# Ten adaLN rows of a two-layer trunk: sum over the partitions by accumulating transfers instead of matmuls with ones

## The chip, the cores and the metric

The kernel runs on one core of a Trainium2 chip. The metric is device time in microseconds (us), the median of the runs. Engines are written PE (TensorE), DVE (VectorE), ACT (ScalarE), POOL (GpSimd) and SP (SyncE). A DMA is issued by an engine, in the order of that engine's program; here SP and POOL issue them.

## The reference

512 tokens of 1024 values pass through two layers; layer 0 mixes tokens by stick-breaking attention, layer 1 by a gMLP, and each is followed by a SwiGLU FFN of width 2816. Around each of these four sub-layers stand two RMS norms, scaled and shifted by rows that are computed from one conditioning vector c:

```python
def ada_modulation(c, w, b):
    m = jax.nn.silu(c) @ w + b
    shift, scale, gate = jnp.split(m, 3, axis=-1)
    ...
for i in range(DEPTH):
    shift, scale, gate = ada_modulation(c, mix_ada_w[i], mix_ada_b[i])
    h = rms_norm(x, mix_pre_g[i]) * (1.0 + scale) + shift
    ...
    x = x + gate * rms_norm(y, mix_post_g[i])
    shift, scale, gate = ada_modulation(c, ffn_ada_w[i], ffn_ada_b[i])
    h = rms_norm(x, ffn_pre_g[i]) * (1.0 + scale) + shift
    y = swiglu(h, ffn_w_gate[i], ffn_w_up[i], ffn_w_down[i])
    x = x + gate * rms_norm(y, ffn_post_g[i])
```

The change concerns the product silu(c) @ w + b: rows of 1024 values (shift, scale, gate), each a sum over 1024 rows of w.

## The kernel before

**Layout of the work.** Everything in fp32 goes through PE as three matmuls of rounded halves (high by high, high by low, low by high; `mm3`). Weights are loaded by SP, their high half wh is rounded by ACT, the low half wl is the difference, by DVE. The split pairs lie in a pool of five (`wpool`), so they are made ahead of their use. There are stages: the v, k and q products with attention in between (to about 205 us), the output projection of attention (to 265), the first FFN's gate and up products (`Ffn.seven`, a seven-product scheme per block), its down projection (`out_proj` with steps = 2; about 490 to 605), the gMLP (`gmlp`, to about 760), and the second FFN (`seven`, then `last`). Between the sub-layers stands `boundary(s, tt, ...)`: for each 128 tokens it multiplies by the row G (gate times post gain), adds to x, multiplies by A ((1 + scale) times pre gain) and adds B (shift), then transposes on PE for the next sub-layer.

**The rows.** Ten rows G, A, B for the boundaries are made while other work runs, by the class `Bg` (L313). For boundary 0 they are G0, A0, B0, made during attention, with their loads issued by POOL; G1 is made in the first FFN's `seven` loop, A1, B1 and G2 in its down projection, A2 there and in the gMLP, B2 in the gMLP, and G3 in the second FFN's `seven` loop; these loads are issued by SP. (The first sub-layer's shift and scale are made at the start in another way.) For one row, `Bg.run` does this: POOL clears a tile acc of 128 x 1024 and the bias row is loaded into its partition 0. Then eight times: 128 rows of w are loaded (rawada, 512 KB) and DVE adds them, each scaled by its silu(c) value, to acc (`ada_stt`, L306, a SCALAR_TENSOR_TENSOR). What is left is the sum of acc over its 128 partitions, wanted on every partition.

**The sum over partitions, before.** In halves of 512 columns, acc is split (acch on ACT, accl on DVE) and two matmuls with a matrix of ones, `ones_r`, add up the partitions and put the sum on all of them at once (L369, L370). For 10 rows that is 10 x 2 x 2 = 40 matmuls. Their results stand in PSUM under the names spare (during attention) and adaps. From there G is multiplied by g, and A becomes (1 + sum) times g, both on DVE, g being a gain row that SP loads broadcast to 128 partitions; B is copied by ACT.

**The order of work.** `Bg.run` is a generator. The host stages call `bg.step()` at fixed places, and each step issues the next piece, so the place in each engine's order is set by hand. During attention PE, DVE and ACT run strictly in written order (`chain`); elsewhere the framework's scheduler places instructions by their dependences, and each engine then issues in order. In `out_proj` with steps the bank of y[0] is needed for adaps: the accumulation of y[0] is broken at k = `mid` = 13, ACT copies its first part to yp, the matmuls with ones of A1, B1, G2 all stand after that place, and DVE adds yp back at the end. From k = 13 a second object, bg2, makes A2. `slot` (L47) gives tiles of 4 KB a partition from a pool of 28.

Of the kernel before, what the change touches and what calls it, by code (L numbers as in the profile page):

```python
# [8 lines left out]
F32 = mybir.dt.float32  # L9
# [16 lines left out]
def trunk(ctx: ExitStack, tc: tile.TileContext, A: dict, out: bass.AP):  # L26
# [2 lines left out]
    consts = ctx.enter_context(tc.tile_pool(name="consts", bufs=1))  # L29
    wraw = ctx.enter_context(tc.tile_pool(name="wraw", bufs=2))  # L30
    wpool = ctx.enter_context(tc.tile_pool(name="wpool", bufs=5))
    adas = ctx.enter_context(tc.tile_pool(name="adas", bufs=1))
    npool = ctx.enter_context(tc.tile_pool(name="npool", bufs=2))
    small = ctx.enter_context(tc.tile_pool(name="small", bufs=4))
    s4 = ctx.enter_context(tc.tile_pool(name="s4", bufs=28))
# [277 lines left out]
    class Bg:  # L313
# [5 lines left out]
        def __init__(self, *parts, slots=False, queue=nc.sync):  # L319
            self.slots = slots  # L320
            self.queue = queue
            self.bank = lambda: bank("adaps", "p")

            self.parts = [
                (n, int(s), int(s) + (n != "G"), {"G": 2, "A": 1, "B": 0}[n]) for n, s in parts
            ]
            self.gen = self.run()
            self.todo = [(s, part, k) for _, _, s, part in self.parts for k in range(KD)]
            self.raws = []
# [8 lines left out]
        def run(self):  # L338
            for name, at, s, part in self.parts:
                acc = slot(F32, name, 1, D)[:, 0, :]  # L340
                ada[name, at] = acc
                nc.gpsimd.memset(acc, 0.0)
                load(acc[0:1, :], A["adab"][s, part], self.queue)
                for k in range(KD):
                    if self.slots:
                        raw = slot(F32, "rawada", 1, D)[:, 0, :]
                        load(raw, A["ada"][s, part, k])
                        yield
                    else:
                        self.ahead(1 + (k + 1 < KD or name != self.parts[-1][0]))  # L350
                        raw = self.raws.pop(0)
                    ada_stt(acc, raw, k)
                    if not self.slots:
                        yield
            for name, at, s, part in self.parts:
                acc = ada[name, at]
                if part:
                    row = A["pre_g"] if part == 1 else A["post_g"]
                    g = slot(F32, "g", 1, D)[:, 0, :]
                    load(g, row[s : s + 1, :].to_broadcast([P, D]))  # L360
                for b in range(2):
                    c = slice(b * 512, (b + 1) * 512)
                    h = adas.tile([P, 512], F32R, tag="acch", name=nm("acch"))
                    l = adas.tile([P, 512], F32R, tag="accl", name=nm("accl"))
                    split(h[:], l[:], acc[:, c])
                    yield
                    yield
                    ps = self.bank()
                    mm(ps[:], ones_r, h[:], True, False, last_tp[0])  # L369
                    mm(ps[:], ones_r, l[:], False, True)  # L370
                    if part == 0:
                        act.activation(acc[:, c], ps[:], AF.Copy)
                    elif part == 1:
                        dve.scalar_tensor_tensor(acc[:, c], ps[:], 1.0, g[:, c], ALU.add, ALU.mult)
                    else:
                        dve.tensor_tensor(acc[:, c], ps[:], g[:, c], ALU.mult)

        def step(self, n=1):

            while n and next(self.gen, self) is not self:  # L380
                n -= 1
            return n

    def rms(part, first=None):

# [107 lines left out]
    def out_proj(s, nk, get_act, wkey, J, bg, hT, nxt=(), pre=None, S=None, steps=0, bg2=None):  # L493

        last = 0 if steps else 3
        mid = min(nk - J, -(-8 * len(bg.parts) // steps) + 1) if steps else None  # L500
        yp = None
        y = [[None, None] for _ in range(NT)]

        def step(k, tt, a, w, halves=(0, 1)):
            for hf in halves:
                if k == 0 or k == mid and tt == last:
                    y[tt][hf] = bank("y", "p" if tt == last else "b")
                mm3(
                    y[tt][hf][:],
                    a[0][:, tt * P : (tt + 1) * P], a[1][:, tt * P : (tt + 1) * P],  # L510
                    w[0][:, 0, hf * 512 : (hf + 1) * 512],
                    w[1][:, 0, hf * 512 : (hf + 1) * 512],
                    k == 0 or k == mid and tt == last, k == nk - 1 or k + 1 == mid and tt == last,
                )

        npre = 0
        if pre is not None:
            npre = len(pre["w"])
            for tt in pre["y"]:
                y[tt] = pre["y"][tt]  # L520
        for k in range(nk - J):
            a = get_act(k)
            w = pre["w"][k] if k < npre else wget(wkey(k))
            for tt in range(NT):
                if k >= npre or tt not in pre["y"]:
                    step(k, tt, a, w)
            bg.step(steps)
            if bg2 is not None and mid is not None and k >= mid:
                bg2.step(1)
            if k + 1 == mid:  # L530
                yp = slot(F32, "yp")
                for hf in range(2):
                    act.activation(yp[:, hf, :], y[last][hf][:], AF.Copy)
                bg.step(99)
        bg.step(99)
        tail = [
            (k, get_act(k), wget(wkey(k), J + 1 if k == nk - J else 0))
            for k in range(nk - J, nk)
        ]
        sqrt_table()  # L540
        xs = {tt: x_load(tt) for tt in range(2)}
        xin = xs.get
        for tt in range(NT):
            for hf in range(2):
                for k, a, w in tail:
                    step(k, tt, a, w, (hf,))
            if tt == last and yp is not None:
                for hf in range(2):
                    dve.tensor_tensor(yp[:, hf, :], y[tt][hf][:], yp[:, hf, :], ALU.add)
                y[tt] = [yp[:, hf, :] for hf in range(2)]  # L550
            if tt < 2:
                boundary(s, tt, y[tt], xin, hT, S, "p" if last == 0 else "b")
                xs[tt + 2] = x_load(tt + 2)
        evacs, late = [], []
        for n, tt in enumerate((2, 3)):
            if nxt:
                evacs.append(nxt[n]())
            late.append(boundary(s, tt, y[tt], xin, hT, S, "p" if tt == 3 else "b"))
        if nxt:
            dve.gate, act.gate = ready[0], last_sqrt[0]  # L560
            late[0][1]()
            evacs.append(nxt[2]())
# [195 lines left out]
    with tc.tile_pool(name="att", bufs=1) as att, tc.tile_pool(name="att2", bufs=6) as att2:  # L758
# [192 lines left out]
        bg.bank = None  # L951
        cur = attend(0)
        for k in range(KD):
            if k % 2 == 0:
# [8 lines left out]
        v_evac(vb, 1)  # L963
        tw = [bank("tw") for _ in range(2)]
        av = bank("av")
        spare = bank("spare")
        bg.bank = lambda: spare
        dve.chain = act.chain = True
        fill(6)
        cur[0](B0)  # L970
# [2 lines left out]
        for i in range(NPAIR):  # L973
# [6 lines left out]
            def rest():  # L980
                n, sums = next(F)
                fill(n)
                bg.step(sums)

            for group, js in zip((LATE, *EARLY), (B31, B2, B0)):
                flip(group, 0)
# [11 lines left out]
                step_v(i - 2)  # L998
        for _ in fgen:
            bg.step(1)  # L1000
        bg.step(99)
        pe["chain"] = dve.chain = act.chain = False

# [14 lines left out]
    class Ffn:  # L1018
# [81 lines left out]
        def run(self, bg0, bg, bg2, steps, nhT, nxt, nS=None):  # L1100
            for f in range(NH):
                self.unit(f, 256, 256)()
            for f in range(NH, KF):
                self.seven(f)()
                if f % 3:
                    bg0.step(1)
            bg0.step(99)
            if self.li == 1:
                return self.last()
            out_proj(  # L1110
                self.s, KF, lambda k: act_split(self.act[k // 2][:, k % 2, :]),
                lambda k: ("wdown", self.li, k), 4, bg, nhT, nxt, None, nS, steps, bg2,
            )


        def last(self):
# [113 lines left out]
            for half in range(2):  # L1230
# [3 lines left out]
                tail = items[-NLAST:] if half else []  # L1234
                while n < len(items) and items[n][0] == half and items[n] not in tail:
                    ahead(n)
                    _, kind, j = items[n]
                    n += 1
                    if kind == "o":
# [77 lines left out]
    def gmlp(bg, hT, nhT, nS, nxt):  # L1317
# [96 lines left out]
                    )  # L1414

        for m in range(KD):
            mix(m)
            sp.append(act_split(u4[m // 2][:, m % 2, :]))
            if m >= 4:
                part(m - 4)  # L1420
# [104 lines left out]
```

## Time and profile before

| what | value |
| --- | --- |
| median of three runs | 1125.85 us (1125.52 to 1125.99) |
| the profiled execution, its own time | 1127.71 us |
| its span in the profile | 1125.9 us |
| mean granted clock of PE | 0.998 |
| PE, DVE, ACT, POOL busy | 98%, 80%, 54%, 4% |
| HBM read, written | 164.43 MB, 8.39 MB |

The span runs from the first to the last instruction; the 1.8 us between it and the execution's time lie around it. The busy shares are means over stages with different limits. A row of the timeline gives start, duration, engine, line, operation, output <- inputs, and in brackets how long the engine had been idle before it and what ended that. A row of the groups gives the count and the shortest, median and longest duration in ns. A row of windows gives, for a stretch of time, each engine's busy us, the granted clock, the share of DMA time and GB/s. A row of DMA issues gives the size and the median us from issue to landing. The chain of waits goes back from the last instruction to whatever released each piece.

### The profile page before, as it was taken

The numbers are of one execution on the slowest core, as the hardware profiler recorded it, in microseconds if no ns is written. First come the engines' busy times: TensorE is split into PE (matmuls) and PEld (weight loads), VectorE is DVE, ScalarE is ACT, GpSimd is POOL, SyncE is SP. The second block draws the span as 40 slices with busy tenths as digits, with TensorE's granted clock in tenths as the row PEclk, the third lists the DMA queues.
The fourth block names the chain that finished last, engine by engine and source line by source line (L and its number), as shares of the span: only waits on it lengthen the run. The fifth ranks groups of instructions, "written<-read, shape, count | busy, mean of one in ns | idle before, by whom it ended". The sixth has DMA issues, their size and how long they took to land.

```text
span 1125.9 us, 18286 instructions
## 1 busy us (share of the span) xinstructions
PE 1105.2 (98%) x7318; PEld 993.6 (88%) x7318; DVE 903.2 (80%) x1161; ACT 603.0 (54%) x977; POOL 39.8 (4%) x71
## 2 busy tenths in 40 slices
PE   6999999999999999999999999999999999999997
PEld 5788878779999999988878988988999999989896
DVE  7777889659988988787687774759988898889986
ACT  7646767647555555562244634437555555556552
POOL 0220111000000000010000000000000000000000
PEclk9999999999999999999999999999999999999999
DMA  9676445353244444368875482333244444223233
GB/s 361 234 216 172 145 144 168 124 187 132 76 149 150 134 132 132 110 215 270 270 255 186 159 298 83 116 113 141 84 151 127 137 132 151 75 76 112 95 94 149
DMA packets 51298, 176.09 MB, mean 156 GB/s; under 512 B 5643, under 2 KB 6155, under 8 KB 50318
## 3 DMA queue, kind: packets, MB, share of 16 engines
q1 hardware_dynamic: 45166, 153.95, 41.4%
q0 software_dynamic: 6048, 20.98, 5.9%
q8 instruction: 57, 0.93, 0.3%
q14 instruction: 27, 0.22, 0.1%
HBM read 164.43 MB, written 8.39 MB: 153 GB/s over the span
## 4 chain that ended last, share of the span: by engine, by line
PE 83%; DMA 8%; DVE 6%; issue 2%; ACT 1%; SPq 0%; POOL 0%; DVEq 0%; POOLq 0%; ACTq 0%
PE r L90 32%; PE y L90 12%; PE X L90 7%; PE v L90 7%; PE gu L90 6%; DMA rawada<-in_ada 5%; PE pqk L90 5%; PE u L90 4%; PE M L90 3%; DMA raw<-in_wdown 1%; PE z L90 1%; PE tw L98 1%; DMA ada<-in_ada0w 1%; PE av L90 1%; PE tp L98 1%
## 5 line engine op out<-in xcount | busy, mean ns | idle before, releaser
L64 ACT ACTIVATE wh<-raw 128x1024 fp32r<-128x1024 f32 (+1 forms) x112 | 116.8, 1051 | 140.9 <-PE y L90 42.0
L64 DVE TENSOR_TENSOR wl<-raw,wh 128x1024 fp32r<-128x1024 f32 (+1 forms) x112 | 134.9, 1211 | 61.9 <-ACT wh L64 61.8
L90 PE MATMUL r<-Sh,wh 128*128 128x256 f32 x608 | 170.2, 280 | 0.2 <-ACT e L64 0.2
L90 PE MATMUL r<-Sh,wl 128*128 128x256 f32 x608 | 170.4, 280 | 0.0
L90 PE MATMUL r<-Sl,wh 128*128 128x256 f32 x608 | 170.1, 280 | 0.0
L90 PE MATMUL y<-wh,as 128*128 128x512 f32 x480 | 153.3, 396 | 0.1
L64 DVE TENSOR_TENSOR wl<-f,wh 128x1024 fp32r<-128x1024 f32 x76 | 92.7, 1220 | 35.8 <-ACT wh L64 35.8
L64 ACT ACTIVATE wh<-f 128x1024 fp32r<-128x1024 f32 x76 | 80.6, 1061 | 67.9 <-PE r L90 65.1
L90 PEld LDWEIGHTS r<-Sh,wh 128*128 128x128 f32 x608 | 114.7, 189 | 0.4 <-ACT e L64 0.4
L90 PEld LDWEIGHTS r<-Sl,wh 128*128 128x128 f32 x608 | 114.6, 188 | 0.0
L90 PEld LDWEIGHTS r<-Sh,wl 128*128 128x128 f32 x608 | 114.6, 188 | 0.0
L90 PEld LDWEIGHTS y<-wh,as 128*128 128x128 f32 x480 | 90.1, 188 | 21.5 <-DVE G L64 0.6
L90 PE MATMUL y<-wl,as 128*128 128x512 f32 x240 | 94.9, 395 | 0.0
L90 PE MATMUL r<-hTh,wh 128*128 128x256 f32 x304 | 88.8, 292 | 0.2 <-DVE gu L64 0.2
L90 PE MATMUL r<-hTl,wh 128*128 128x256 f32 x304 | 84.8, 279 | 0.0
L90 PE MATMUL r<-hTh,wl 128*128 128x256 f32 x304 | 80.1, 280 | 0.0
L90 PE MATMUL X<-wh,as 128*128 128x512 f32 (+1 forms) x272 | 76.3, 356 | 0.0
L64 ACT ACTIVATE e<-r 128x256 f32<-128x256 f32 x114 | 43.4, 382 | 51.6 <-PE r L90 51.2
L90 PEld LDWEIGHTS r<-hTh,wh 128*128 128x128 f32 x304 | 57.2, 188 | 5.4 <-DVE gu L64 1.3
L90 PE MATMUL r<-hTh,b 128*128 128x256 f32 x304 | 60.7, 282 | 0.0
L64 ACT ACTIVATE wh<-rawx 128x1024 fp32r<-128x1024 f32 x38 | 40.4, 1063 | 35.9 <-PE r L90 30.8
L90 PEld LDWEIGHTS r<-hTl,wh 128*128 128x128 f32 x304 | 57.3, 188 | 0.1
(240 smaller groups left out, 2844.7 us busy)
## 6 DMA issues: line engine op xcount, KB each, us to landing
rawada<-in_ada SPq DMA_DIRECT2D x56, 512.0 KB, 5.1
raw<-in_wdown SPq DMA_DIRECT2D x44, 512.0 KB, 4.1
rawy<-in_wy SPq DMA_DIRECT2D x38, 512.0 KB, 3.6
rawx<-in_wx SPq DMA_DIRECT2D x38, 512.0 KB, 4.5
rawada<-in_ada POOLq DMA_DIRECT2D x24, 512.0 KB, 4.5
raw<-in_wqk SPq DMA_DIRECT2D x16, 512.0 KB, 4.6
ada<-in_ada0w SPq DMA_DIRECT2D x7, 1026.0 KB, 10.8
raw<-in_wgu SPq DMA_DIRECT2D x12, 512.0 KB, 3.6
```

The costliest lines, as they stand in the source:

```text
L64: b = f(*a, **k)
L90: b = nc.tensor.matmul(o, l, r, start=start, stop=stop, skip_group_check=True)
L98: last_tp[0] = nc.tensor.transpose(o, i, ident)
```

## The change

After the eighth sum of a row a generator `total` is put on a list `trees`. It adds the upper half of acc's partitions to the lower half by a DMA that accumulates at its destination, seven times (64, 32, 16, 8, 4, 2, 1 partitions), each waiting for the one before; loads the 4 KB gain row and does the product with it on one partition (1 x 1024) on DVE (for A and G); stores the row to DRAM; and reads it back to 128 partitions. POOL issues all of these transfers. A function `grow` moves every tree by one step; it is called at each step of `Bg` and at some other places (in attention, in the `seven` loop, in `last`, in the gMLP's `mix` loop). The splits, the 40 matmuls, their evacuations, the broadcast loads of g, and the break of y[0] go away; bg2 still begins at k = 13.

```diff
-            for name, at, s, part in self.parts:
-                acc = ada[name, at]
...
-                    load(g, row[s : s + 1, :].to_broadcast([P, D]))
...
-                    split(h[:], l[:], acc[:, c])
-                    yield
-                    yield
-                    ps = self.bank()
-                    mm(ps[:], ones_r, h[:], True, False, last_tp[0])
-                    mm(ps[:], ones_r, l[:], False, True)
...
                     ada_stt(acc, raw, k)
+                    if k == KD - 1:
+                        trees.append(total(acc, s, part))
...
             while n and next(self.gen, self) is not self:
+                grow()
                 n -= 1
...
+    def total(acc, s, part):
+
+        n = P // 2
+        while n:
+            nc.gpsimd.dma_start(out=acc[0:n, :], in_=acc[n : 2 * n, :], accum_op=ALU.add)
+            yield
+            n //= 2
+        if part:
+            g = slot(F32, "g", 1, D)[:, 0, :]
+            load(g[0:1, :], A["pre_g" if part == 1 else "post_g"][s : s + 1, :], nc.gpsimd)
+            yield
+            if part == 1:
+                dve.scalar_tensor_tensor(acc[0:1, :], acc[0:1, :], 1.0, g[0:1, :], ALU.add, ALU.mult)
+            else:
+                dve.tensor_tensor(acc[0:1, :], acc[0:1, :], g[0:1, :], ALU.mult)
+        row = dram.tile([1, D], F32, tag="row", bufs=4, name=nm("row"))
+        nc.gpsimd.dma_start(out=row[:], in_=acc[0:1, :])
+        yield
+        nc.gpsimd.dma_start(out=acc, in_=row[:].to_broadcast([P, D]))
+
+    def grow(n=1):
+
+        while n and trees:
+            trees[:] = [t for t in trees if next(t, trees) is not trees]
+            n -= 1
...
-        mid = min(nk - J, -(-8 * len(bg.parts) // steps) + 1) if steps else None
-        yp = None
+        begin = 8 * len(bg.parts) // steps + 1 if steps else None
...
-            if k + 1 == mid:
-                yp = slot(F32, "yp")
-                for hf in range(2):
-                    act.activation(yp[:, hf, :], y[last][hf][:], AF.Copy)
-                bg.step(99)
```

Where instructions move. First DVE at the end of attention, before: two sums of B0 (B_1496), the scans ga, and the k that the last scores of attention use.

```order
L64 SCALAR_TENSOR_TENSOR B_1496<-rawada_1692,sc,B_1496 128x1024
L64 SCALAR_TENSOR_TENSOR ga_1725<-ga_1725,tri 128x256 x2
L64 SCALAR_TENSOR_TENSOR B_1496<-rawada_1718,sc,B_1496 128x1024
L64 SCALAR_TENSOR_TENSOR ga_1759<-ga_1759,tri 128x512 x2
L64 TENSOR_TENSOR k_1770<-pqk_1705,k_1770 64x512 x2
```

And after, the same place (B_1505 is B0's acc, A_1052 is A0's, g_1737 its gain row):

```order
L63 SCALAR_TENSOR_TENSOR B_1505<-rawada_1707,sc,B_1505 128x1024
L63 SCALAR_TENSOR_TENSOR ga_1743<-ga_1743,tri 128x256 x2
L63 SCALAR_TENSOR_TENSOR B_1505<-rawada_1734,sc,B_1505 128x1024
L63 SCALAR_TENSOR_TENSOR A_1052<-A_1052,g_1737 1x1024
L63 SCALAR_TENSOR_TENSOR ga_1781<-ga_1781,tri 128x512 x2
L63 TENSOR_TENSOR k_1792<-pqk_1721,k_1792 64x512 x2
```

A0's product with its gain row stands between the last sum of B0 and the last scans, ahead of k. G0's stands in the same way behind the last sum of A0.

Second, POOL's queue at the same time, before: the last loads of rawada and then the first store of x by the boundary.

```order
L107 DMA rawada_1663<-in_ada 128x1024
L107 DMA rawada_1692<-in_ada 128x1024
L107 DMA rawada_1718<-in_ada 128x1024
L429 DMA xd_2160<-x_2118 128x1024
```

And after, from the load that answers to rawada_1663 on:

```order
L106 DMA rawada_1677<-in_ada 128x1024
L367 DMA A_1052<-A_1052 4x1024
L106 DMA rawada_1707<-in_ada 128x1024
L367 DMA A_1052<-A_1052 2x1024
L106 DMA g_1737<-in_pre_g 1x16x64
L367 DMA A_1052<-A_1052 1x16x64
L106 DMA rawada_1734<-in_ada 128x1024
L367 DMA B_1505<-B_1505 64x1024
L379 DMA row_1774<-A_1052 16x1x64
L367 DMA B_1505<-B_1505 32x1024
L381 DMA A_1052<-row_1774 128x1024
```

The last steps of A0's tree stand between the loads of rawada, and B0's tree begins behind the last load.

Third, PE in the first FFN's down projection at the change from k = 12 (wh_5546) to k = 13 (wh_5585), before; y_5208 is the second half of y[3], y_5188 the first half of y[1] (the matmuls of y[0] for k = 13 stand further on):

```order
L90 MATMUL y_5208<-wh_5546,as_5656 128x512
L90 MATMUL y_5208<-wl_5547,as_5656 128x512
L90 MATMUL y_5208<-wh_5546,as_5656 128x512
L90 MATMUL adaps_5698<-acch_5691,ones 128x512
L90 MATMUL adaps_5698<-accl_5692,ones 128x512
L90 MATMUL y_5188<-wh_5585,as_5744 128x512
L90 MATMUL y_5188<-wl_5586,as_5744 128x512
```

And after, where wh_5584 is the weight of k = 13, y_5178 the second half of y[3] and y_5150 the first half of y[0]:

```order
L89 MATMUL y_5178<-wh_5543,as_5661 128x512
L89 MATMUL y_5178<-wl_5544,as_5661 128x512
L89 MATMUL y_5178<-wh_5543,as_5661 128x512
L89 MATMUL y_5150<-wh_5584,as_5694 128x512
L89 MATMUL y_5150<-wl_5585,as_5694 128x512
L89 MATMUL y_5150<-wh_5584,as_5694 128x512
```

The pairs on ones are gone; what stood behind them follows the matmuls of k = 12 directly.

More of the change, by code (lines that the diff above doesn't have):

```diff
@@ L31, in trunk @@
     wpool = ctx.enter_context(tc.tile_pool(name="wpool", bufs=5))
-    adas = ctx.enter_context(tc.tile_pool(name="adas", bufs=1))
     npool = ctx.enter_context(tc.tile_pool(name="npool", bufs=2))
@@ L321, in __init__ @@
             self.queue = queue
-            self.bank = lambda: bank("adaps", "p")
             self.parts = [
@@ L352, in run @@
                     ada_stt(acc, raw, k)
+                    if k == KD - 1:
+                        trees.append(total(acc, s, part))
                     if not self.slots:
                         yield
-            for name, at, s, part in self.parts:
-                acc = ada[name, at]
-                if part:
-                    row = A["pre_g"] if part == 1 else A["post_g"]
-                    g = slot(F32, "g", 1, D)[:, 0, :]
-                    load(g, row[s : s + 1, :].to_broadcast([P, D]))
[L361 to L364, printed above, removed]
-                    split(h[:], l[:], acc[:, c])
-                    yield
-                    yield
-                    ps = self.bank()
-                    mm(ps[:], ones_r, h[:], True, False, last_tp[0])
-                    mm(ps[:], ones_r, l[:], False, True)
[L371 to L376, printed above, removed]
@@ L378, in step @@
         def step(self, n=1):
             while n and next(self.gen, self) is not self:
+                grow()
                 n -= 1
             return n
+    trees = []
+    def total(acc, s, part):
[16 more added lines that the diff above has]
+        nc.gpsimd.dma_start(out=acc, in_=row[:].to_broadcast([P, D]))
@@ L505, in step @@
             for hf in halves:
-                if k == 0 or k == mid and tt == last:
+                if k == 0:
                     y[tt][hf] = bank("y", "p" if tt == last else "b")
@@ L512, in step @@
                     w[1][:, 0, hf * 512 : (hf + 1) * 512],
-                    k == 0 or k == mid and tt == last, k == nk - 1 or k + 1 == mid and tt == last,
+                    k == 0, k == nk - 1,
                 )
@@ L527, in out_proj @@
             bg.step(steps)
-            if bg2 is not None and mid is not None and k >= mid:
+            if steps == 0:
+                grow()
+            if bg2 is not None and k >= begin:
                 bg2.step(1)
-            if k + 1 == mid:
-                yp = slot(F32, "yp")
-                for hf in range(2):
-                    act.activation(yp[:, hf, :], y[last][hf][:], AF.Copy)
-                bg.step(99)
         bg.step(99)
@@ L546, in out_proj @@
                     step(k, tt, a, w, (hf,))
[L547 to L550, printed above, removed]
             if tt < 2:
@@ L950, in trunk @@
         zb = [bank("z") for _ in range(2)]
-        bg.bank = None
         cur = attend(0)
@@ L965, in trunk @@
         av = bank("av")
-        spare = bank("spare")
-        bg.bank = lambda: spare
         dve.chain = act.chain = True
@@ L982, in rest @@
                 fill(n)
-                bg.step(sums)
+                if bg.step(sums):
+                    grow()
             for group, js in zip((LATE, *EARLY), (B31, B2, B0)):
@@ L1000, in trunk @@
             bg.step(1)
+            grow()
         bg.step(99)
@@ L1106, in run @@
                     bg0.step(1)
+                else:
+                    grow()
             bg0.step(99)
@@ L1236, in last @@
                     ahead(n)
+                    grow()
                     _, kind, j = items[n]
@@ L1416, in gmlp @@
         for m in range(KD):
+            grow()
             mix(m)
```

## The prediction

> **What bounds the kernel now.** I read the page first, for the share of each engine and the 40 slices:
>
> ```profile
> PE 1105.2 (98%) x7318; PEld 993.6 (88%) x7318; DVE 903.2 (80%) x1161; ACT 603.0 (54%) x977; POOL 39.8 (4%) x71
> ...
> PE   6999999999999999999999999999999999999997
> ```
>
> TensorE is busy for 1105.2 of 1125.9 us, in every slice but the first and the last. So there are two ways to gain: issue fewer matmuls, or remove some of the 20.7 us in which PE is idle. Next I read who ends those idle times, in the view of waits for PE:
>
> ```profile
> PE sc L90 <- ACT sc L64: 3.0, 1, 3.0
> PE adaps L90 <- ACT acch L64: 2.7, 1, 2.7
> PE v L90 <- ACT hTh L64: 2.6, 3, 1.5
> PE y L90 <- DVE k L64: 2.6, 1, 2.6
> ```
>
> Two of them belong to this change. The 2.7 us are a wait of a matmul that the change removes; the 2.6 us are a wait for DVE, to which the change gives work. Third, the price of a matmul. The groups of the removed ones, and a long piece of PE in the chain that ended last:
>
> ```profile
> L90 PE MATMUL adaps<-acch,ones x14: 387/395/501, 470.0 to 1000.6; 128*128 128x512 f32 x14
> ...
> L90 PE MATMUL adaps<-accl,ones x14: 387/393/403, 470.2 to 1000.8; 128*128 128x512 f32 x14
> ```
>
> ```profile
> L90 PE MATMUL spare<-acch,ones x6: 388/434/502, 210.9 to 230.3; 128*128 128x512 f32 x6
> ...
> L90 PE MATMUL spare<-accl,ones x6: 392/393/422, 211.1 to 231.1; 128*128 128x512 f32 x6
> ```
>
> ```profile
> 231.48 20.98 PE y L90 x90
> ```
>
> The groups hold 14 + 14 + 6 + 6 = 40 matmuls of about 0.39 us each. But the chain passes 90 matmuls of the same shape in 20.98 us, 0.233 us each: consecutive ones overlap, and the duration counts the overlap twice. What a removed matmul gives back on a full PE is the spacing.
>
> **What is removed.** 40 × 0.233 = 9.3 us. By the mean durations it would be 14 × 0.395 + 14 × 0.393 + 6 × 0.434 + 6 × 0.393 = 16.0, which I do not take.
>
> Then the wait of 2.7. It is one matmul in the output projection of the first FFN, and beside it what ACT did:
>
> ```profile
> 569.92 0.50 PE L90 MATMUL adaps<-acch,ones 128*128 128x512 f32 x1 [2.66 <-ACT acch L64]
> ```
>
> ```profile
> 568.29 1.06 ACT L64 ACTIVATE wh<-raw 128x1024 fp32r<-128x1024 f32 x1 [1.59 <-DMA raw<-in_wdown]
> 569.25 0.61 ACT L64 ACTIVATE acch<-A 128x512 fp32r<-128x512 f32 x1
> ```
>
> ACT's acch stood behind a weight split that waited 1.59 us for its load. The pool of split weights holds five pairs and is filled ahead, so that split is for a weight some k later; the y matmuls behind the stalled one belong to k = 13, whose weight was split before: they waited only because PE issues in order. Without the ones matmul nothing holds PE there, so 2.66 us go whole. What could be late next is the weight behind that slow load, up to five k further on, a k being 24 matmuls or 5.6 us; that is the first rival. The y[0] accumulation broken at k = 13, its two copies on ACT and two additions on DVE go too; PE did not wait for those, so nothing for them.
>
> The splits (acch on ACT, accl on DVE) and the evacuations go from engines that PE does not wait for at those places: nothing.
>
> **What is added on DVE.** A and G each get one operation on 1x1024. One partition or 128, the free size is the same, so I price it by the 128x1024 rows of DVE. The last 40 us of attention, where two of them stand:
>
> ```profile
> 162.04 1.28 DVE L64 SCALAR_TENSOR_TENSOR A<-rawada,sc,A 128x1024 f32<-128x1024 f32 x1
> ...
> 173.68 1.23 DVE L64 TENSOR_TENSOR wl<-raw,wh 128x1024 fp32r<-128x1024 f32 x1 [0.41 <-ACT wh L64]
> ...
> 178.99 1.41 DVE L64 TENSOR_TENSOR k<-pqk,k 64x512 fp32r<-64x512 f32 x2 [0.39 <-ACT k L64]
> ...
> 198.40 1.28 DVE L64 SCALAR_TENSOR_TENSOR B<-rawada,sc,B 128x1024 f32<-128x1024 f32 x1 [1.78 <-DMA rawada<-in_ada]
> 199.60 2.33 DVE L64 TENSOR_TENSOR_SCAN ga<-ga,tri 128x512 f32<-128x512 f32 x2
> 201.94 1.39 DVE L64 TENSOR_TENSOR k<-pqk,k 64x512 fp32r<-64x512 f32 x2
> ```
>
> ```profile
> 203.48 0.77 PE L90 MATMUL y<-wh,o 128*128 128x512 f32 x1 [2.63 <-DVE k L64]
> ```
>
> Here DVE runs in written order and PE waits 2.63 us for its k. G's operation stands right behind the sum at 162.04, A's right behind the sum at 198.40, ahead of the scan at 199.60 and of k. Each takes 1.2 us. The first is partly absorbed by idle times of 0.41 and 0.39 us that end with ACT; about 0.8 us stay. (The 1.78 us before 198.40 absorb nothing: that load is issued when a DVE sum frees its buffer, so it moves with DVE.) The second is not absorbed. So the wait of 2.63 grows by 2.0 us. Bounds: 0, if a short row is cheap or the load comes earlier; and 4, if a longer pause also slows what follows. For the latter there is this:
>
> ```profile
> 203.48 3.66 PE y L90 x9
> ```
>
> ```profile
> 200.00:210.00 10.00, 7.37 (x33) 5.91 (x32) 8.49 (x10) 4.52 (x7) 0.00 (x0) 0.83 0.79 255
> 210.00:220.00 10.00, 10.00 (x70) 7.85 (x68) 7.52 (x10) 7.82 (x14) 0.00 (x0) 1.00 0.03 9
> 500.00:595.00 95.00, 92.21 (x396) 73.80 (x395) 70.92 (x73) 28.41 (x37) 0.95 (x1) 1.00 0.81 268
> ```
>
> (The last three columns are the granted clock, the DMA share and GB/s.) After the 2.63 us of idle nine matmuls took 3.66 us in place of 9 × 0.233 = 2.1, and the granted clock of those 10 us is 0.83: 1.56 us of slow matmuls are paid already. The wait of 2.66 us at 569.92 cost no clock (1.00 in the row of its stage, 500 to 595). A longer pause could bring one more such 1.56 us, hence the 4. The Trainium skill, TensorE: Matmul & The Clock Gate, Part 1, has the clock halve after an idle window of about 3.4 us and return after about as long a busy one; by that, a pause of 4.6 us costs at most 1.7 us (an estimate from that page), and the trace agrees in size, while its pause of 2.63 us, below that figure, had the clock down already. The other three G and three A and B operations stand where PE does not wait for DVE: nothing.
>
> **What is added on the DMA queues.** Each of the ten parts now has seven accumulating transfers, each waiting for the one before, a row store and a read-back. No accumulating transfer is in the trace. The nearest rows:
>
> ```profile
> rawada<-in_ada SPq DMA_DIRECT2D x56, 512.0 KB, 5.1
> ...
> xd<-x POOLq DMA_DIRECT2D x12, 512.0 KB, 2.9
> ...
> g<-in_post_g SPq DMA_DIRECT2D x4, 512.0 KB, 7.7
> ...
> after<-V POOLq DMA_DIRECT2D x4, 508.0 KB, 10.6
> ...
> A<-in_adab POOLq DMA_DIRECT2D x1, 4.0 KB, 2.4
> B<-in_adab POOLq DMA_DIRECT2D x1, 4.0 KB, 2.1
> ```
>
> A step moves 256 KB down to 4 KB: between 2.1 us (a single row) and 10.6 us (the only moves from SBUF to SBUF here, five queued at once with the DMA engines full). I take 2.5, nearest to the uncrowded rows. With a store of 2.9 and a broadcast read of 7.7, a tree takes 7 × 2.5 + 10.6 = 28 us. It is hidden as long as nobody needs the row by then. The tightest place is B of the first boundary, whose last sum ends at 198.40 + 1.28 = 199.7, and:
>
> ```profile
> 251.00 1.28 DVE L64 SCALAR_TENSOR_TENSOR t<-t,r,B 128x1024 f32<-128x1024 f32 x1
> ```
>
> With the 12 spare matmuls gone (2.8 us) and 2.0 added, it is needed at about 250.2, and the tree starts at about 200.5: 49.7 us, less 10.6, leaves 5.6 us a step. At 2.5 the tree ends 21 us early.
>
> POOL issues in order, so loads of rawada stand behind steps. The closest is the last of them:
>
> ```profile
> 188.29 0.54 POOL L107 DMA_DIRECT2D rawada<-in_ada  x1 [4.75 <-DVE B L64]
> 193.14 0.53 POOL L107 DMA_DIRECT2D rawada<-in_ada  x1 [4.31 <-DVE B L64]
> ```
>
> Between these two now come step 6 of A, a row load and step 7, which waits for step 6: 1.6 us of issues and one step's landing in 4.31 us of idle. At 2.5 they fit, above about 3.8 they push the load, and with it the 2.63 us wait. Nothing at my price.
>
> **The sum.** On the profiled execution's 1127.7: −9.3 − 2.7 + 2.0 = −10.0, so 1117.7. It stands 1.86 us above the median of the runs, and the same change on the median, 1125.85, gives 1115.9.
>
> **Rivals.**
>
> (1) Contention in the FFN's output projection. From 500 to 595 the DMA engines are 0.81 busy at 268 GB/s, 25.5 MB. Three trees and four read-backs, less two broadcast loads of g, add 3.6 − 1.0 = 2.6 MB, or 4.1 if accumulation also reads its destination: 10 to 15 us of transfers, against 18 us of idle share. If that idle share is not usable (PE already waited for a late load at 568), the weights come late by up to 15 us, of which a lead of one to two k (5.6 to 11 us) that is not used up already covers, I judge, more than half: 6 us come back, so −4.0, 1121.9. For it: the 1.59 us wait for in_wdown. Against: PE itself is full there. The Trainium skill, DMA: Bandwidth & Descriptors, Issuing engines are not separate DMA queues, says that transfers started by SP and by GpSimd share the same 16 engines and interleave; by that the move to POOL's queue protects the weights from nothing, which leaves it at this price.
>
> (2) Slower: the accumulating steps cost what the after<-V rows cost. At 10.4 a step B's tree takes 73 + 10.6 = 83.4 us against 49.7, and the first boundary waits 34 us; PE issues the transpositions of that boundary in order, so it waits too: 1115.9 + 34 = 1150. It eats the whole gain from 5.6 + 10/7 = 7.0 us a step. For it: it is the only SBUF-to-SBUF row. Against: those transfers were queued together in a full stretch, B's tree runs from 200, and from 210 to 220 the DMA engines are 0.03 busy.
>
> (3) The 40 matmuls give their durations: −16.0 − 2.7 + 2.0, so 1109.2. Against: the spacing of 0.233.
>
> (4) The gain is eaten to within the bound in attention: if steps of 4.5 to 6 us each hold a rawada load back by 1 to 2 us at several places, the wait of 2.63 grows by 8 to 10 instead of 2, about 1124.
>
> **How the numbers follow.** Forecast 0.60, with its own range 1113.6 (nothing added on DVE) to 1118 (4 us); rival 1 0.16; rival 2 0.13; rival 3 0.04; rival 4 0.07. The range reaches from 1112.5, a little under the forecast's lower end for the clock lost at 203, to 1124, which takes in rival 1 and its 2 us of attention stall. A measurement of this kernel tells a difference of about 0.2%, 2.25 us, from none. Faster by more: forecast, rivals 1 and 3, 0.80; within: 0.07; slower: 0.13.
>
> **What would show it.** Forty matmuls fewer, none on ones; no wait of PE in 560 to 570; PE's wait for k near 205 at 4 to 5 us; steps of an accumulating transfer at 2 to 3 us; no wait of the first boundary for A or B. The forecast is wrong if a step takes over 4 us, if PE waits for wl or wh in 570 to 600, or if the wait for k stays at 2.6.

## The result, and the profile after

The changed kernel took 1134.19 us (median of 7 runs, 1130.96 to 1140.14); the kernel before, in the same sessions, 1125.85 (1122.23 to 1127.48). The ratio is 1.0085, 95% interval 1.0069 to 1.0100: 0.85% slower, where 1115.9 was forecast, a gain of 0.9%. The profiled execution took 1130.96 us with a span of 1129.2, the shortest of the seven, so its trace shows somewhat less loss than the median has.

The first line of the page already says that the matmuls went and PE was left idle instead:

```profile
PE 1100.0 (97%) x7278; PEld 989.4 (88%) x7278; DVE 887.4 (79%) x1132; ACT 587.7 (52%) x949; POOL 110.8 (10%) x168
```

There are 40 matmuls fewer and 5 us less of PE work, while the span grew by 3.3. The waits of PE after (us in total, times, longest):

```profile
PE y L89 <- DVE k L63: 6.8, 1, 6.8
PE y L89 <- DVE wl L63: 5.7, 1, 5.7
...
PE tp L97 <- DVE t L63: 1.7, 1, 1.7
PE y L89 <- ACT wh L63: 0.7, 1, 0.7
```

The wait for acch is gone, as said. The wait for k has grown from 2.6 to 6.8, and three waits are new: for wl, t and wh. The windows show where, and that each of the two long waits is followed by slow matmuls (third column from the end: granted clock):

```profile
200.00:220.00 20.00, 13.22 (x68) 10.94 (x69) 13.31 (x14) 7.48 (x14) 4.31 (x6) 0.74 0.55 144
580.00:600.00 20.00, 16.09 (x68) 12.36 (x66) 10.71 (x9) 3.19 (x3) 4.24 (x6) 0.96 0.92 297
600.00:620.00 20.00, 15.79 (x59) 12.44 (x60) 13.97 (x20) 8.49 (x18) 4.03 (x5) 0.78 0.76 234
```

**The end of attention.** Four rows of POOL, then DVE, then PE:

```profile
189.92 0.84 POOL L367 DMA_DIRECT2D A<-A  x1
190.47 0.82 POOL L106 DMA_DIRECT2D g<-in_pre_g  x1
194.58 0.78 POOL L367 DMA_DIRECT2D A<-A  x1 [3.29 <-DMA A<-A]
195.20 0.74 POOL L106 DMA_DIRECT2D rawada<-in_ada  x1
```

```profile
200.68 1.28 DVE L63 SCALAR_TENSOR_TENSOR B<-rawada,sc,B 128x1024 f32<-128x1024 f32 x1 [3.32 <-DMA rawada<-in_ada]
201.88 1.21 DVE L63 SCALAR_TENSOR_TENSOR A<-A,g 1x1024 f32<-1x1024 f32 x1
203.01 2.32 DVE L63 TENSOR_TENSOR_SCAN ga<-ga,tri 128x512 f32<-128x512 f32 x2
205.37 1.39 DVE L63 TENSOR_TENSOR k<-pqk,k 64x512 fp32r<-64x512 f32 x2
```

```profile
206.90 0.77 PE L89 MATMUL y<-wh,o 128*128 128x512 f32 x1 [6.78 <-DVE k L63]
```

Step 7 of A0's tree waits on POOL until step 6 has landed, 194.58 − 189.92 = 4.7 us after its issue began, and the last load of rawada, queued behind it, goes out at 195.20 for 193.14 before. Of these 2.06 us the step made about 0.9, its 4.7 less the 3.8 for which the prediction had room; the other 1.1 are DVE's own, whose sum that frees the load's buffer starts at 192.56 in place of 191.45. DVE waits 3.32 us for it (1.78 before), then does A0's product, 1.21 us, ahead of the scans and k. The chain has nine y matmuls behind the wait:

```profile
206.90 4.18 PE y L89 x9
211.08 1.97 PE z L89 x8
```

The nine y took 4.18 us for 2.1 at full speed; before it was 3.66. With the eight z behind them these 17 matmuls took 6.15 us, for 3.66 + 1.14 = 4.80 before.

**The first FFN's down projection.** DVE stands in order at A1's product, which waits for A1's tree; some 45 us later PE waits for the splits behind:

```profile
550.98 1.21 DVE L63 SCALAR_TENSOR_TENSOR A<-A,g 1x1024 f32<-1x1024 f32 x1 [6.63 <-DMA A<-A]
552.12 1.27 DVE L63 SCALAR_TENSOR_TENSOR G<-rawada,sc,G 128x1024 f32<-128x1024 f32 x1
...
598.72 2.60 DVE L63 SCALAR_TENSOR_TENSOR A<-rawada,sc,A 128x1024 f32<-128x1024 f32 x2 [3.96 <-DMA rawada<-in_ada]
601.25 2.36 DVE L63 TENSOR_TENSOR wl<-raw,wh 128x1024 fp32r<-128x1024 f32 x2
```

```profile
596.28 0.50 PE L89 MATMUL y<-wh,as 128*128 128x512 f32 x1 [0.69 <-ACT wh L63]
602.52 0.79 PE L89 MATMUL y<-wl,as 128*128 128x512 f32 x1 [5.74 <-DVE wl L63]
```

A2's last sum ends at 601.3 in place of 594.8, and the wl that PE needs stands behind it. The transfers themselves, by size (KB each, median us to landing):

```profile
rawada<-in_ada SPq DMA_DIRECT2D x56, 512.0 KB, 5.5
...
G<-row POOLq DMA_DIRECT2D x4, 512.0 KB, 7.2
...
A<-A POOLq DMA_DIRECT2D x3, 256.0 KB, 4.7
B<-B POOLq DMA_DIRECT2D x3, 256.0 KB, 5.4
...
A<-A POOLq DMA_DIRECT2D x3, 128.0 KB, 6.2
...
G<-G POOLq DMA_DIRECT2D x4, 4.0 KB, 2.4
```

By these medians a step takes 2.4 to 6.2 us, not 2.5; rawada takes 5.5, for 5.1. What the DMA engines do beside a step shows in its time: the last four steps of B0 (32 to 4 KB), from 217 to 231 us with the engines 0.05 busy, landed in 2.9, 2.7, 2.3 and 2.0 us; those of A1, of the same sizes and from 516 to 549 us with the engines 0.87 busy, in 4.7, 3.3, 4.5 and 2.5.

Where the loss arises can be read from when PE begins the first transpositions of a boundary, in us, in both kernels and in the first experiment (no trees at all):

| kernel | boundary 0 | boundary 1 | boundary 2 | end of the span |
| --- | --- | --- | --- | --- |
| before | 252.34 | 611.24 | 761.53 | 1125.9 |
| after | 254.35 | 617.27 | 766.27 | 1129.2 |
| e1, no trees | 249.13 | 600.47 | 749.29 | 1112.6 |

Of the 16.6 us between after and e1, 5.2 arise before boundary 0, 11.6 between boundaries 0 and 1, and nothing (−0.2) behind.

### The profile page after: what moved, and what is told of

It reads as the page before. It is cut to its first block, busy times and chain, and to the rows that moved or that the text cites. A ratio compares the mean times of both kernels' runs of the same rounds, so it can differ in the third digit from the quotient of the medians.

```text
span 1129.2 us, 18328 instructions
## 1 busy us (share of the span) xinstructions
PE 1100.0 (97%) x7278; PEld 989.4 (88%) x7278; DVE 887.4 (79%) x1132; ACT 587.7 (52%) x949; POOL 110.8 (10%) x168
## 4 chain that ended last, share of the span: by engine, by line
PE 80%; DMA 9%; DVE 5%; issue 3%; ACT 1%; POOL 1%; SPq 0%; DVEq 0%; POOLq 0%; ACTq 0%
PE r L89 33%; PE y L89 8%; PE X L89 7%; PE v L89 7%; PE gu L89 6%; PE pqk L89 5%; DMA rawada<-in_ada 4%; PE u L89 4%; PE M L89 3%; DMA A<-A 2%; PE z L89 1%; PE av L89 1%; DMA raw<-in_wdown 1%; PE tw L97 1%; PE tp L97 1%
## 5 line engine op out<-in xcount | busy, mean ns | idle before, releaser
L89 PEld LDWEIGHTS y<-wl,as 128*128 128x128 f32 x240 | 45.7, 191 | 16.8 <-DVE wl L63 6.3
L367 POOL DMA_DIRECT2D G<-G x28 | 22.6, 807 | 385.5 <-DVE G L63 320.6
```

What stands on the lines that cost most here:

```text
L89: b = nc.tensor.matmul(o, l, r, start=start, stop=stop, skip_group_check=True)
L367: nc.gpsimd.dma_start(out=acc[0:n, :], in_=acc[n : 2 * n, :], accum_op=ALU.add)
```

## The experiments

The theory: the 40 matmuls and the wait for acch are worth what was said; the loss comes from two places, attention (A0's steps and product in the way of a load and of k) and the down projection. For the second, two causes compete: DVE standing in order at a product that waits for a tree, or the transfers taking DMA time from the loads. All edits are to the changed kernel; each was compared with the kernel before on its own chip (1125.3 to 1125.8 there), so a difference between two experiments can be off by 0.5 us.

**e1, the trees left out.**

```diff
-                    if k == KD - 1:
-                        trees.append(total(acc, s, part))
```

> The trees are left out altogether (no sum over partitions, no product with the gain row, so the rows G, A and B are wrong). Theory: the 40 matmuls and the wait of 2.66 us are worth about 12 us, and all the loss of the changed kernel comes from what replaces them; then about 1114 us, no wait of PE for k above 3 us and none for wl in the first FFN's down projection. Rival: the removed matmuls were worth much less than their spacing of 0.233 us (other work takes their place); then 1118 to 1122.

1113.51 us (1111.57 to 1114.41), ratio 0.9881 (0.9858 to 0.9904). What the change removes is worth 12.3 us; the sum of the prediction had 9.3 + 2.7 = 12.0. The page has it in PE's busy time, 9.2 us less than the 1105.2 before:

```profile
PE 1096.0 (99%) x7278; PEld 987.0 (89%) x7278; DVE 881.5 (79%) x1125; ACT 588.3 (53%) x949; POOL 39.8 (4%) x71
```

The rival falls. All of the changed kernel's 20.7 us above this come from the trees.

**e2, the product on GpSimd.**

```diff
-            if part == 1:
-                dve.scalar_tensor_tensor(acc[0:1, :], acc[0:1, :], 1.0, g[0:1, :], ALU.add, ALU.mult)
-            else:
-                dve.tensor_tensor(acc[0:1, :], acc[0:1, :], g[0:1, :], ALU.mult)
+            if part == 1:
+                nc.gpsimd.tensor_scalar(acc[0:1, :], acc[0:1, :], 1.0, None, ALU.add)
+            nc.gpsimd.tensor_tensor(acc[0:1, :], acc[0:1, :], g[0:1, :], ALU.mult)
```

> The product with the gain row is done by GpSimd on the one partition instead of by DVE; everything else as in the changed kernel. Theory A (DVE in order, waiting for a tree, is what hurts): in the first FFN's down projection the 6.63 us in which DVE waits at the product of A1 go, the sums of G2 and A2 and the wl behind them come earlier, PE's wait of 5.7 us for wl goes, and in attention the wait for k falls from 6.8 to about 5.6; about 1122 to 1125 us. Rival B (the transfers themselves hurt: bytes and shared DMA engines): the wait for wl stays at 4 us or more; 1130 to 1133 us.

1138.87 us (1134.22 to 1141.96), ratio 1.0108 (1.0076 to 1.0141): worse than the changed kernel, and outside the ranges of A and of B. PE's waits:

```profile
PE y L89 <- DVE k L63: 9.7, 1, 9.7
PE y L89 <- DVE wl L63: 4.9, 1, 4.9
```

The wait for wl stayed, as rival B had it. But the edit brought a cost of its own, as POOL's rows and the DVE row beside them show:

```profile
560.35 2.77 POOL L375 TENSOR_SCALAR A<-A 1x1024 f32<-1x1024 f32 x1 [3.77 <-DMA A<-A]
563.20 2.38 POOL L376 TENSOR_TENSOR A<-A,g 1x1024 f32<-1x1024 f32 x1
```

```profile
563.31 3.36 DVE L63 SCALAR_TENSOR_TENSOR G<-rawada,sc,G 128x1024 f32<-128x1024 f32 x1 [3.53 <-DMA rawada<-in_ada]
```

GpSimd needs 5.2 us for A's product, the steps of B1's tree queue behind it, and a sum on DVE that ran at the same time took 3.36 us for 1.28; four more DVE operations that ran beside a product on GpSimd took 3.0 to 3.4. So e2 does not tell A from B; e10 does.

**e3, A0's last steps held.** A0's tree is set aside at the fifth sum of B0 and taken up again at the eighth, and every step is ordered behind the last load of rawada that POOL has issued (last_ada is set there).

```diff
                     ada_stt(acc, raw, k)
+                    if (name, at) == ("B", 0) and k in (4, KD - 1):
+                        held[:], trees[:] = trees[:], held[:]
...
-            nc.gpsimd.dma_start(out=acc[0:n, :], in_=acc[n : 2 * n, :], accum_op=ALU.add)
+            b = nc.gpsimd.dma_start(out=acc[0:n, :], in_=acc[n : 2 * n, :], accum_op=ALU.add)
+            order(b, last_ada[0])
```

> In attention alone the last steps of A0's tree are issued behind the last load of rawada, and so its product on DVE stands behind k. Theory: the load is no longer held back by about 2 us and the product of 1.2 us no longer stands ahead of k, so PE's wait for k falls from 6.8 to about 3.4 us, the slow-clock matmuls behind it from 6 to 3.7 us; about 5 us less than the changed kernel, 1127 to 1130 us. Rival: the load is late for DMA reasons (the trees' transfers slow it), then the wait falls only by the 1.2 us of the product, 1132 to 1133.

1131.17 us (1128.71 to 1132.85), ratio 1.0042 (1.0024 to 1.0060): 3.0 us less than the changed kernel, not 5. In attention the wait did what was said; POOL, DVE and PE at the same place:

```profile
194.65 0.53 POOL L106 DMA_DIRECT2D rawada<-in_ada  x1 [4.14 <-DVE B L63]
195.18 0.86 POOL L373 DMA_DIRECT2D A<-A  x1
```

```profile
198.73 1.28 DVE L63 SCALAR_TENSOR_TENSOR B<-rawada,sc,B 128x1024 f32<-128x1024 f32 x1 [0.88 <-DMA rawada<-in_ada]
```

```profile
203.84 0.76 PE L89 MATMUL y<-wh,o 128*128 128x512 f32 x1 [2.84 <-DVE k L63]
```

The load waits for DVE alone, and PE's wait is 2.84 us. But the slow matmuls behind it did not go from 6 to 3.7 us: the same 17 took 4.18 + 2.11 = 6.29. Boundary 0 begins at 251.43, 2.9 us earlier. In the seven traces with A0 held (e3 and e5 to e10) it begins at 248.1 to 252.4, against 249.13 without any trees, so A0's place was most of the loss in attention. In this execution the gain is lost again at boundary 1, where PE waited 3.98 us for t in place of 1.69 (the chain goes back to a load of the gMLP's weights that took 7.0 us, whose split stood in ACT's order ahead of the boundary's work), and behind it, where matmuls ran slow: boundary 2 comes at 766.39, for 766.27 in the changed kernel.

**e4, no trees in the down projection.**

```diff
-                    if k == KD - 1:
+                    if k == KD - 1 and (name, at) not in (("A", 1), ("B", 1), ("G", 2)):
```

> The trees and products of A1, B1 and G2, those that run in the first FFN's down projection, are left out (these rows are wrong); all others stay. Theory: the waits of PE between 590 and 620 us (5.74 for wl, 0.69 for wh, 1.69 for t, and slow clock behind them) come from these trees, so they go: 9 to 11 us less than the changed kernel, about 1124 us. Rival: part of that loss comes from A2's eight sums, which now follow G2's directly in the same stretch; then a wait of 2 to 5 us stays, 1127 to 1130.

1121.85 us (1120.05 to 1122.19), ratio 0.9963 (0.9944 to 0.9983). PE's two longest waits are now:

```profile
PE y L89 <- DVE k L63: 8.4, 1, 8.4
PE tp L97 <- DVE x L63: 3.1, 3, 1.2
```

The waits between 590 and 620 for wl, wh and t are gone, and A2's sums alone leave none; the rival falls. By the medians the three trees cost 12.3 us, and what is left above e1, 8.3 us, belongs to the other seven, attention's above all: in this trace boundary 0 begins at 256.78, 7.65 us after e1's, and the whole span is 7.8 us longer. The wait for k varies by execution: 6.78 and 8.45 us in two traces of the same instructions up to there, in which the last load of rawada took 5.4 and 7.3 us.

**e5, A2's sums later.** On e3.

```diff
-            if bg2 is not None and k >= begin:
-                bg2.step(1)
```

> The held A0 of e3, and A2's sums are no longer begun in the first FFN's down projection but with B2's in the gMLP (eight loads of 512 KB fewer in that stretch; the trees of A1, B1, G2 stay there). Theory C (DMA engines full, so each rawada load takes longer, A2's sums stretch out, and the last wl stand behind them in DVE's order): PE's waits for wl and t between 590 and 620 us go, boundary 1 comes about 10 us earlier than in e3; 1118 to 1122 us. Rival D (the trees hold something else back, POOL's queue or the rows A1 and B1 themselves): the wait for t stays and the time stays above 1127.

1127.94 us (1125.48 to 1131.81), ratio 1.0020 (1.0001 to 1.0039), not the 1118 to 1122 of theory C. Boundary 1 comes at 601.46, 12.7 us before e3's 614.15, and in the down projection no wait above 0.4 us is left. But boundary 2 comes at 761.65, 160 us behind it, where the changed kernel took 149. The chain and the window there:

```profile
691.53 4.58 DMA A<-A
696.14 1.21 DVE A L63
698.12 1.18 DVE wl L63
```

```profile
700.00:720.00 20.00, 17.03 (x102) 16.42 (x101) 17.70 (x22) 12.56 (x15) 4.25 (x5) 0.72 0.69 216
```

A2's product, waiting for A2's tree, now stands in DVE's order ahead of the gMLP's layer norm, and PE's pauses behind it have slow matmuls again. The wait had moved. The pauses themselves are 3.0 us in four pieces, none over 1.63; the granted clock behind them was 0.50 from 710 to 724, about 7 us lost by that clock, so most of the 11 us is slow matmuls and not waiting.

**e6, small steps.** On e3; small is true for A1, B1 and G2.

```diff
+            m = 1 if small else n
-            b = nc.gpsimd.dma_start(out=acc[0:n, :], in_=acc[n : 2 * n, :], accum_op=ALU.add)
+            b = nc.gpsimd.dma_start(out=acc[0:m, :], in_=acc[n : n + m, :], accum_op=ALU.add)
```

> The held A0 of e3; the seven steps of the trees of A1, B1 and G2 each move one partition of 4 KB, 28 KB a tree for 508 (these three rows are wrong); steps, store and read-back stay. Theory C by bytes: with 1.4 MB fewer moved, and as much fewer read at the destination, the wait for wl falls from 4.9 to 2 us or less; 1122 to 1126. Rival E (the number of waiting transfers and the read-backs count, not the steps' bytes): 1129 to 1132.

1118.26 us (1116.74 to 1124.48), ratio 0.9936 (0.9909 to 0.9963): 12.9 us less than e3 with the same transfers in the same order, only smaller. No wait for wl is left; 4.0 us for t remain in the trace, which is of the longest of the five executions. Rival E falls: the bytes that the steps move count. In the trace they count in two ways. The loads of rawada land in 4.9 us, for 5.4 in e3. And A1's tree itself is shorter, from the first to the last of its seven issues 25.4 us (513.36 to 538.77) for 29.8 in e3 (514.01 to 543.85), so that DVE waits less at A1's product; e3, then e6:

```profile
546.83 1.21 DVE L63 SCALAR_TENSOR_TENSOR A<-A,g 1x1024 f32<-1x1024 f32 x1 [5.70 <-DMA A<-A]
```

```profile
542.04 1.21 DVE L63 SCALAR_TENSOR_TENSOR A<-A,g 1x1024 f32<-1x1024 f32 x1 [2.76 <-DMA A<-A]
```

A2's last sum starts at 586.97 in place of 595.28, and 4.8 of these 8.3 us are there when A1's product starts. So the 12.9 us are not the loads' alone; DVE's order has a part in them, which e10 tests.

**e7, no read-back; e8, copies.** On e3, for A1, B1 and G2.

```diff
-        nc.gpsimd.dma_start(out=acc, in_=row[:].to_broadcast([P, D]))
+        nc.gpsimd.dma_start(out=acc[0:1, :], in_=row[:])
```

> The held A0 of e3; the rows of A1, B1 and G2 are read back to one partition only, 4 KB for 512 (these rows are wrong on the others). Theory C by bytes: 1.5 MB fewer, about half of what the trees add, the waits for wl and t fall by about half; 1125 to 1128. If the read-back with its 128 readers of one row is what is dear: 1119 to 1122. If the steps are what is dear: 1130 to 1131.

1125.97 us (1123.48 to 1127.32), ratio 0.9998 (0.9984 to 1.0012): 5.2 us less than e3, in the range for "half". But 1.5 MB fewer are worth 5.2 us here and 1.4 MB fewer 12.9 in e6, so the number of bytes alone does not set the gain. Here DVE's wait at A1's product was no shorter (9.06 us), nor was PE's for wl (5.0 us in two); only that for t fell, to 1.7.

```diff
-                b = nc.gpsimd.dma_start(out=acc[0:n, :], in_=acc[n : 2 * n, :], accum_op=ALU.add)
+                b = nc.gpsimd.dma_start(out=acc[0:n, :], in_=acc[n : 2 * n, :])
```

> The held A0 of e3; the steps of the trees of A1, B1 and G2 copy the upper half over the lower without accumulating (these rows are wrong). If accumulation is dear because the destination is read as well, a step lands in about 3 us for 5 and the waits shrink; 1124 to 1127. If it is only the bytes moved and the full engines, no change: 1130 to 1132.

1128.32 us (1124.51 to 1133.47), ratio 1.0023 (1.0001 to 1.0044). Its median lies between the two ranges and is 2.9 us below e3's, its runs overlap e3's, and in its trace PE's waits for wl are no shorter (7.6 us in two). A1's seven issues took 29.3 us (511.01 to 540.26), for 29.8 with accumulation. So accumulating as such explains at most a small part.

**e10 and e9, later products.** Outside attention the product is put two steps of the trees later and ordered behind the DVE instruction that was written last.

```diff
-            yield
+            for _ in range(1 + lag):
+                yield
+            prev = dve.prev
             if part == 1:
...
+            order(b, prev)
```

e10 is this on e3:

> The held A0 of e3 with the later products, but A2's sums begun in the down projection as in the changed kernel. If DVE's wait for A1's tree (5.7 us in e3) is what makes the wl late, PE's waits between 590 and 620 fall by half or more; 1122 to 1126. If the pace of the loads is what makes them late, as e2 says, no change: 1129 to 1132.

1123.89 us (1119.93 to 1129.56), ratio 0.9996 (0.9980 to 1.0013): 7.3 us less than e3 with the same transfers. Five products (G1, A1, G2, A2, G3) stand later in DVE's order, and with them, on POOL, the row stores and read-backs that follow. At A1's product:

```profile
543.91 1.21 DVE L63 SCALAR_TENSOR_TENSOR A<-A,g 1x1024 f32<-1x1024 f32 x1 [1.18 <-DMA A<-A]
```

DVE waits 1.18 us for A1's tree for 5.70 in e3, and PE's wait for wl is 3.3 us for 4.9 (the trace is of the shortest of ten executions). So theory A holds as well, and e2 had hidden it. What the later stores and read-backs add to it was not tested apart.

e9 is this on e5:

> e5 (A0 held, A2's sums in the gMLP), and outside attention the product with the gain row is put later in DVE's order (two steps of the trees later, and behind the DVE instruction written last), so that DVE does not stand waiting for a tree. In e5 the 10 us saved in the down projection were lost again in the gMLP, where A2's product waits for A2's tree ahead of the layer norm. If that wait is the cause, boundary 2 comes about 148 to 150 us after boundary 1 in place of 160, and the whole takes 1116 to 1119 us, faster than the kernel before. Rival: the DMA engines (0.85 busy from 640 to 680 in e5) hold the gMLP's weights back whatever DVE's order; 1124 to 1128.

1116.69 us (1113.85 to 1117.92), ratio 0.9926 (0.9911 to 0.9940), the fastest kernel here that computes everything: 0.74% under the kernel before. PE's waits:

```profile
PE y L89 <- DVE k L63: 4.4, 1, 4.4
PE sc L89 <- ACT sc L63: 2.8, 1, 2.8
```

No wait for wl is left, boundaries 1 and 2 stand 148.9 us apart (604.11 and 753.03), and 3.2 us remain above e1, by the trace nearly all in attention: boundary 0 begins at 252.35, 3.2 us after e1's.

## Why the prediction was wrong

- **What is removed** was right. 9.3 for the matmuls by their spacing and 2.7 for the wait make 12.0; e1 measured 12.3, and 9.2 of PE's busy time. Rival 3, with the durations, would have been 18.7.
- **The price of a step** failed. "I take 2.5, nearest to the uncrowded rows" held where the DMA engines were idle (B0's last steps, 2.0 to 2.9); A0's steps ran beside engines 0.55 to 0.77 busy and A1's beside 0.87, and there a step took 2.5 to 8.7 us. The prediction itself had named the point: "above about 3.8 they push the load, and with it the 2.63 us wait. Nothing at my price." A step took 4.7, and the load was held by about 0.9 us.
- **The added wait in attention**, "+2.0", became +4.2 (6.78 for 2.63): 1.2 for A0's product, as said, 0.75 by which DVE was later ahead of the load, 1.5 more of DVE's wait for the load (3.32 for 1.78), and 0.7 by which PE came to the wait earlier in this execution. The 0.75 match the 0.8 that was said for G0's product by luck: 1.2 less the two idle times of 0.41 and 0.39 is 0.4. Of the 1.5, 0.9 are the step. The slow matmuls behind the wait cost 1.35 us more (6.15 for 4.80), about the 1.56 of the bound, but wait and clock together, 5.5 us, passed the bound of 4 in this trace.
- **"The other three G and three A and B operations stand where PE does not wait for DVE: nothing"** failed, and this is the larger error. PE did not wait there before; but A1's product waits for its tree in DVE's order, 6.63 us, and G2's sums, A2's sums and the splits of the last weights stand behind it. Putting the products later gave 7.3 us (e10, measured on e3).
- **Rival 1**, contention, had a part of the mechanism and the place with a chance of 0.16, but its 6 us were too few: the three trees cost 12.3 (e4). From 500 to 595 the DMA engines moved no more bytes than before (25.07 MB for 25.50) and were yet busier (0.86 for 0.81), so they worked at a lower rate; why is not shown. Left out were the product's wait, the slow clock behind PE's pause (0.78 from 600 to 620), and that the loads of rawada are issued only as sums free their buffers, so that every longer landing slows all that follow. Smaller steps gave most (e6, 12.9, with a shorter wait of DVE in it), smaller read-backs some (e7, 5.2), plain copies little (e8). These parts overlap and do not add up to 12.3: each edit alone may free the path.
- **Rival 2** placed its loss at boundary 0; B0's tree ended with its read-back issued at 230.75 and nobody waited for it. Its sign was right, its place wrong.
- **The lower end** of the forecast, 1113.6 with nothing added on DVE, is 0.3 under its own sum (1125.85 − 12.0); nothing hangs on it.

What stays open: how the 12.3 us of the three trees divide between DVE's order and the pace of the loads, since e6 changed both. And why the changed kernel's runs spread over 9 us is not traced; the wait for k differs by 1.7 us between two traces, and the slow matmuls behind such a wait by 2.8 (below).

## What to carry to other kernels

Here work taken off a full engine gave back its spacing (9.2 us for 9.3); what replaces it must be priced at the load of its own stretch, not at the row of an idle one. A chain of dependent transfers is free only if its stretch has room for the transfers and nothing stands in order behind a member of it: look at each queue and each engine for the instruction that waits for the chain, and put that one behind the work that is due. Here the same change became a gain of 0.74% when A0's last steps were held behind the load, the consumers of the trees were moved later and one part's loads left the full stretch.

## What the runs showed of the hardware

- A chain of dependent transfers beside DMA engines 0.84 to 0.88 busy got only 15% shorter with smaller ones: seven steps of 4 KB took 25.4 us, seven of 256 to 4 KB 29.8 (A1, e6 and e3). The Trainium skill, DMA: Bandwidth & Descriptors, Anatomy of one DMA, gives a transfer about 2.0 us of fixed time and the bytes at 436 GB/s, an estimate of 2.6 us for 256 KB; the trace of the changed kernel had medians of 4.2 to 5.4.
- An elementwise GpSimd operation on one partition of 1024 values took 2.3 to 2.8 us (1.21 on DVE) and stretched the DVE sum beside it from 1.28 to 3.36 (e2). The Trainium skill, GPSIMD Engine Reference, Specifications, says that GpSimd shares its SBUF interfaces with VectorE, with contention for instructions with two SBUF inputs; the trace agrees, the sum having two.
- How long matmuls run slow behind a pause of PE did not follow the length of the pause. The same 17 matmuls (nine y, eight z) behind the wait for k took 6.15 us after a pause of 6.78 us (the changed kernel), 6.29 after 2.84 (e3), 4.80 after 2.63 (before) and 3.47, full speed, after 3.18 (e8). So one and the same order of instructions could lose nothing or 2.8 us there. The windows of e3, then of e8, with the granted clock third from the end:

```profile
200.00:220.00 20.00, 17.16 (x93) 13.71 (x92) 14.36 (x16) 10.99 (x19) 6.03 (x9) 0.83 0.55 140
```

```profile
200.00:220.00 20.00, 16.82 (x106) 13.35 (x105) 14.09 (x15) 11.50 (x20) 6.38 (x9) 1.00 0.51 135
```
